# DeltaNet: the keys' sums of squares from their transposed copy; last FFN: 512 tokens in one PSUM bank

## The chip, the cores and the metric

The program runs on one core of one Trainium2 chip. The metric is device time in microseconds (us), the median of the runs shown. An execution taken by the hardware profiler gives the views quoted here: PE is TensorE (matmuls), PEld its weight loads, DVE is VectorE, ACT is ScalarE, POOL is GpSimd, SP is SyncE, which issues the DMAs. L12 is line 12 of the kernel before.

## The reference, cut to what matters

512 tokens of width 1024 pass through a first block of two layers (retention, sparse attention, gated MLP, each layer with a feed-forward network, FFN) and a second block of two layers. In the second block the first layer mixes with a gated DeltaNet over the 512 tokens and 256 context tokens, the second with differential attention; each is followed by an FFN. The context is dropped after the first of these layers, so the last FFN sees the 512 tokens alone. Two pieces matter here:

```
def _l2norm(x):
    return xf * lax.rsqrt(jnp.sum(jnp.square(xf), axis=-1, keepdims=True) + RMS_EPS)

# DeltaNet, per head of 128 channels, q, k, v after a 5-tap convolution and silu:
q = _l2norm(q) * (DN_DK ** -0.5);  k = _l2norm(k)

# FFN, hidden width 2816:
def _swiglu(h, w_gate, w_up, w_down):
    return (jax.nn.silu(h @ w_gate) * (h @ w_up)) @ w_down
```

## The kernel before, in words

All activations lie transposed, channels on the 128 partitions and tokens along the free axis. Every large product is made of three matmuls (`mm3`, L208 to L212): both operands are split into a high and a low fp32r part, and hi·hi, lo·hi and hi·lo are summed in PSUM. `gemm_b` (L243 to L255) loads and splits one unit of weights (`load_split`, L196 to L206: a DMA, a copy on ACT, a subtraction on DVE), takes one PSUM bank for each segment of tokens in `segs`, and runs over the segments and, inside, over the contraction in steps of 128. A segment of 256 tokens is a matmul of 256 columns, one of 512 tokens a matmul of 512.

**The last FFN** (`ffn2`, L1408 to L1463, called by `rest` with `halves`, two segments of 256 tokens). The 2816 hidden channels are 22 chunks of 128, in three groups of 8, 8 and 6. `gate_up` (L1415) makes one chunk: gate and up products, 8 contraction steps each, then tanh on ACT (L1429), two operations on DVE (L1430, L1431), the high part on ACT (L1432) and the low part on DVE (L1433), all once for each segment. `down` (L1435) makes one of the 8 output chunks from a group's hidden chunks and adds it into x (L1439). The first four chunks are made half by half, since each half's input comes out of a layer norm of its own, and the third group's `down` is made half by half, since the layer norm behind it wants each half complete. In between, chunks 4 to 21 and the `down` of groups 1 and 2 run over both halves in one call, as two segments. This phase has six PSUM banks for the products and two for statistics. In the built program's memory layout the FFN's input tiles (`ghhi`, `ghlo`) begin at multiples of 64 bytes, as do those of the first block's FFN (`fhhi`, `fhlo`) and all hidden tiles (`ahi`, `alo`, `bhi`, `blo`); the inputs of the second block's first FFN (`ahhi`, `ahlo`) begin 32 bytes past one.

**The DeltaNet's projection** (`project` in `dn`, L1020 to L1057), once for each of 8 heads and for k, q and v in this order: products, a copy to SBUF, a 5-tap convolution on DVE (L1036), silu by tanh on ACT (L1037, tile `cth`) and one operation on DVE (L1038), which leaves `kT`, `qT` or `vT`, channels by 768 tokens with 4 columns of padding. For q and k the squares are taken on ACT (L1042, tile `sq`, which shares the one buffer of `cth`), and for each of six token tiles a matmul against a column of ones sums them over the partitions into one PSUM bank (L1045, `pss`); DVE adds 1e-6 (L1047, `vvk`, `vvq`). For k and v six transposes on TensorE, three to a bank, and two copies, one on DVE and one on ACT (L442, L276, L274), make the token-major `ktok` and `vtok`. `pss` and the transposes share one PSUM bank (tag "t"). `blocks` (L1059) takes the reciprocal roots on POOL (`rk`, `rq`, L279) and builds the decay-weighted products, `invert` the triangular inverses, `scan` the recurrence. Two heads are projected ahead of the one that is scanned.

The order of instructions on each engine is set when the program is built, by the Tile framework's scheduler, from the order of the code, the waits and a priority that the weight loads and `invert` carry. Each engine then runs its list in order.

Of the kernel before, what the change touches and what calls it, by code (L numbers as in the profile page):

```python
# [14 lines left out]
F32 = mybir.dt.float32  # L15
F32R = mybir.dt.float32r
AF = mybir.ActivationFunctionType
OP = mybir.AluOpType
AX = mybir.AxisListType
# [3 lines left out]
P = 128  # L23
T = 512
# [163 lines left out]
class Kern:  # L188
# [723 lines left out]
    def dn(self, then):  # L912


        tc, nc, a = self.tc, self.nc, self.a
        nt, n, PAD = 6, NALL, 4
        both = ((0, NCTX, 1, a["ctxT"]), (NCTX, T, 0, self.xd[:]))
        W_ = n + PAD
        col0 = lambda t: t * P + (PAD if t >= 2 else 0)
        tsl = lambda t: slice(col0(t), col0(t) + P)  # L920
        segs = ((0, NCTX), (NCTX, T))
        with ExitStack() as pools:
# [17 lines left out]
            with tc.tile_pool(name="dg", bufs=1, reuse_waits="tile") as dg:  # L940
# [23 lines left out]
                y, e, z, z2, p, g = (dg.tile([P, nt, 16], F32, name=x) for x in ("y", "e", "z", "z2", "p", "g"))  # L964
# [19 lines left out]
                for t in range(nt):  # L984
                    for d in range(2):
                        nc.tensor.matmul(pc[:, (t * 2 + d) * 8:(t * 2 + d) * 8 + 8], tri[d], g[:, t, d * 8:d * 8 + 8],
                                         start=True, stop=True)
# [18 lines left out]
            dq = pools.enter_context(tc.tile_pool(name="dq", bufs=1, reuse_waits="tile"))  # L1006
            dr = pools.enter_context(tc.tile_pool(name="dr", bufs=1, reuse_waits="tile"))
# [12 lines left out]
            def project(hd):  # L1020

                hh = {}
                for nm in "kqv":
                    c = {"q": 0, "k": 8, "v": 16}[nm] + hd
                    pss_ = self.gemm_b(hk, KD, a["dn_in"][c], segs)
                    s = dq.tile([P, W_], F32, name=f"{nm}T", bufs=DNB[nm])
                    hh[nm + "T"] = s
                    th = dr.tile([P, W_], F32, name="cth", bufs=1)
                    cp = cps[flip[0] % 2]
                    flip[0] += 1  # L1030
                    for (s0, w), ps in zip(segs, pss_):
                        c0 = col0(s0 // P)
                        nc.scalar.activation(cp[:, c0 + 2:c0 + 2 + w], ps[:, :w], AF.Copy)
                    nc.scalar.activation(s, cp[:, 2:2 + W_], AF.Copy, scale=self.conv[:, c, 2:3])
                    for j in (0, 1, 3, 4):
                        nc.vector.scalar_tensor_tensor(s, cp[:, j:j + W_], self.conv[:, c, j:j + 1], s, op0=OP.mult, op1=OP.add)  # L1036
                    nc.scalar.activation(th, s, AF.Tanh, scale=0.5)  # L1037
                    nc.vector.scalar_tensor_tensor(s, th, 1.0, s, op0=OP.add, op1=OP.mult)  # L1038
                    if nm != "v":

                        sq = dr.tile([P, W_], F32, name="sq", tag="cth", bufs=1)
                        nc.scalar.activation(sq, s, AF.Square, scale=0.5)  # L1042
                        pq = self.ps("t", "pss")
                        for t in range(nt):
                            nc.tensor.matmul(pq[:, t:t + 1], sq[:, tsl(t)], self.ones[:, 0:1], start=True, stop=True)  # L1045
                        vv = dq.tile([P, nt], F32, name=f"vv{nm}", bufs=3)
                        nc.vector.tensor_scalar(vv, pq[:, :nt], 1e-6, None, op0=OP.add)  # L1047
                        hh["vv" + nm] = vv
                    if nm != "q":
                        tok = dq.tile([P, nt, P], F32, name=f"{nm}tok", bufs=DNB[nm + "tok"])  # L1050
                        hh[nm] = tok
                        for t0 in (0, 3):
                            pt = self.ps("t", "qkvt")
                            for t in range(3):
                                self.tpose(pt[:, t * P:(t + 1) * P], s[:, tsl(t0 + t)])
                            self.copy(tok[:, t0:t0 + 3].rearrange("p t c -> p (t c)"), pt[:, :3 * P])
                return hh  # L1057

            def blocks(hh, hd):  # L1059
# [211 lines left out]

            ah = DNB["ahead"]
            hs = {i: project(i) for i in range(ah)}
            w = blocks(hs[0], 0)
            invert(w)
            zs = {i: z_gate(i) for i in range(ZA)}
            for hd in range(8):
                w0 = w
                for step in ORD:
                    if step == "z" and hd < 8 - ZA:  # L1280
                        zs[hd + ZA] = z_gate(hd + ZA)
                    elif step == "s":
                        with (tc.high_priority() if HP & 2 else nullcontext()):
                            scan(hs[hd], hd, w0, zs.pop(hd))
                    elif step == "b" and hd < 7:
                        with (tc.high_priority() if HP & 4 else nullcontext()):
                            w = blocks(hs[hd + 1], hd + 1)
                    elif step == "i" and hd < 7:
                        with (tc.high_priority() if HP & 1 else nullcontext()):
                            invert(w)  # L1290
                    elif step == "p" and hd + ah < 8:
                        hs[hd + ah] = project(hd + ah)
# [115 lines left out]
    def ffn2(self, l, n, x, f, fp, norm):  # L1408

        nc, a = self.nc, self.a  # L1410
        streams, h = f["streams"], f["h"]
        hk = lambda k: (h[0][:, k], h[1][:, k])
        act = {}

        def gate_up(c, part, by_k=False):  # L1415
            segs = tuple(p[:2] for p in part)
            ws = a["f_gate"][l, c], a["f_up"][l, c]
            if by_k:
                pg, pu = self.gemm_k(hk, KD, ws, segs)
            else:  # L1420
                pg, pu = (self.gemm_b(hk, KD, w, segs) for w in ws)
            if c not in act:
                act[c] = [fp.tile([P, n], F32R, name=f"b{s}", tag=f"b{s}", bufs=10) for s in ("hi", "lo")]
            hi, lo = act[c]
            for (s0, w, _), g_, u_ in zip(part, pg, pu):
                s = slice(s0, s0 + w)
                th = fp.tile([P, 512], F32, name="bth", bufs=2)
                g = fp.tile([P, 512], F32, name="bg", bufs=2)
                nc.scalar.activation(th[:, :w], g_[:, :w], AF.Tanh, scale=0.5)  # L1429
                nc.vector.scalar_tensor_tensor(g[:, :w], th[:, :w], 1.0, g_[:, :w], op0=OP.add, op1=OP.mult)  # L1430
                nc.vector.scalar_tensor_tensor(g[:, :w], g[:, :w], 0.5, u_[:, :w], op0=OP.mult, op1=OP.mult)  # L1431
                nc.scalar.activation(hi[:, s], g[:, :w], AF.Copy)  # L1432
                nc.vector.tensor_tensor(lo[:, s], g[:, :w], hi[:, s], op=OP.subtract)  # L1433

        def down(gi, c0, cn, m, part):  # L1435
            ps = self.gemm_b(lambda k: act[c0 + k], cn, a[f"f_down{gi}"][l, m], tuple(p[:2] for p in part))
            for (s0, w, st), p in zip(part, ps):
                xs = x[:, m, s0:s0 + w]
                nc.vector.scalar_tensor_tensor(xs, p[:, :w], self.mod[:, l, st, 40 + m:41 + m], xs, op0=OP.mult, op1=OP.add)  # L1439
                yield xs  # L1440

        for gi, (c0, cn) in enumerate(GROUPS):
            if gi == 0:

                for p in streams:
                    for c in range(NLEAD):
                        gate_up(c, [p], c == 0)

                ag = f["ag"]
                for k in range(KD):  # L1450
                    nc.scalar.activation(x[:, k], x[:, k], AF.Identity, scale=ag[:, 0, k:k + 1], bias=ag[:, 1, k:k + 1])
            for c in range(max(c0, NLEAD), c0 + cn):
                gate_up(c, streams)
            if gi < 2:
                for m in range(KD):
                    for _ in down(gi, c0, cn, m, streams):
                        pass
            else:
                for i, p in enumerate(streams):
                    st = self.ln_begin(p[1], i)  # L1460
                    for m in range(KD):
                        for xs in down(gi, c0, cn, m, [p]):
                            self.ln_add(st, xs)  # L1463
                    norm(i, self.ln_end(st))
# [246 lines left out]
```

## Time and profile before

| what | us |
|---|---|
| median of 3 runs (lowest, highest) | 3587.92 (3581.33, 3589.96) |
| the profiled execution | 3586.47 |
| its span, from the first to the last instruction | 3584.7 |
| PE busy | 3429.6 |
| DVE busy | 2183.5 |
| ACT busy | 1450.8 |

The profiled execution lies 1.45 us under the median; 1.77 us of it lie outside the span. Matmuls are pipelined, so a matmul's own duration overlaps the next one's; the step from one matmul's start to the next is what it costs in a dense stream. "Granted clock" is the share of TensorE's full clock, 1.00 for 2.4 GHz and 0.50 for 1.2 GHz.

### The profile page before, as it was taken

How to read it: one execution, taken by the hardware profiler on the slowest of the kernel's cores; microseconds unless marked ns; L12 is line 12 of the kernel's file. 1: busy time of each engine (PE TensorE's matmuls, PEld its weight loads, DVE VectorE, ACT ScalarE, POOL GpSimd, SP SyncE). 2: the span in 40 equal slices, each digit the busy share in tenths (PEclk: the TensorE clock that was granted, in tenths of full speed). 3: DMA queues.
4: the chain of work that ended last, by engine and by line, in shares of the span. 5: the costliest groups of instructions: out<-in, count | busy, mean ns of one | idle time of the engine just before them, and what ended most of it. 6: DMA issues, size and time to landing. Idle time of an engine off the chain costs nothing.

```text
span 3584.7 us, 57586 instructions
## 1 busy us (share of the span) xinstructions
PE 3429.6 (96%) x23334; PEld 2890.0 (81%) x23334; DVE 2183.5 (61%) x4509; ACT 1450.8 (40%) x2736; POOL 119.2 (3%) x125
## 2 busy tenths in 40 slices
PE   8999999989999999999999899999998999989998
PEld 7677888876778888787888777888888877679998
DVE  4556995545569844586778676333247666674446
ACT  4442322335333222556666755112126444452224
POOL 1000000010000000000100000000000000000000
PEclk9998999999989999999999799999999999999999
DMA  5113563330125833211111232111123211133223
GB/s 194 50 52 102 188 222 123 113 96 34 57 101 200 268 113 121 92 54 34 54 47 33 65 104 100 65 65 60 65 81 112 74 42 46 58 124 107 95 94 108
DMA packets 119859, 341.60 MB, mean 95 GB/s; under 512 B 16865, under 2 KB 33521, under 8 KB 119080
## 3 DMA queue, kind: packets, MB, share of 16 engines
q1 hardware_dynamic: 119592, 337.92, 28.5%
q8 instruction: 183, 3.00, 0.3%
q14 instruction: 84, 0.69, 0.1%
HBM read 326.26 MB, written 14.75 MB: 95 GB/s over the span
## 4 chain that ended last, share of the span: by engine, by line
PE 79%; DVE 8%; ACT 5%; DMA 3%; issue 2%; POOL 2%; SPq 0%; POOLq 0%; DVEq 0%; ACTq 0%
PE gb L210 17%; PE gb L212 17%; PE gb L211 17%; DMA wada<-ada_w 2%; PE S L1562 2%; PE ga L210 2%; PE ga L212 2%; DVE wlo L205 2%; PE ga L211 2%; PE S L611 1%; PE da L212 1%; PE da L211 1%; PE da L210 1%; ACT whi L204 1%; PE po L637 1%
## 5 line engine op out<-in xcount | busy, mean ns | idle before, releaser
L204 ACT ACTIVATE whi<-wraw 128x1024 fp32r<-128x1024 f32 (+3 forms) x513 | 490.6, 957 | 1204.6 <-PE gb L211 881.0
L205 DVE TENSOR_TENSOR wlo<-wraw,whi 128x1024 fp32r<-128x1024 f32 (+3 forms) x513 | 561.6, 1096 | 388.7 <-ACT whi L204 384.3
L210 PE MATMUL gb<-fhhi,whi 128*128 128x512 f32 x704 | 275.8, 392 | 3.2 <-ACT fhhi L317 3.2
L212 PE MATMUL gb<-fhhi,wlo 128*128 128x512 f32 x704 | 275.8, 392 | 2.0 <-DVE wlo L205 1.8
L211 PE MATMUL gb<-fhlo,whi 128*128 128x512 f32 x704 | 275.5, 391 | 0.0
L210 PE MATMUL gb<-ahhi,whi 128*128 128x256 f32 (+1 forms) x672 | 226.8, 337 | 0.7 <-ACT whi L204 0.7
L211 PE MATMUL gb<-ahlo,whi 128*128 128x256 f32 (+1 forms) x672 | 226.5, 337 | 0.0
L212 PE MATMUL gb<-ahhi,wlo 128*128 128x256 f32 (+1 forms) x672 | 226.3, 337 | 0.0
L211 PE MATMUL gb<-blo,whi 128*128 128x256 f32 (+1 forms) x704 | 218.3, 310 | 0.0
L210 PE MATMUL gb<-bhi,whi 128*128 128x256 f32 (+1 forms) x704 | 218.2, 310 | 0.0
L212 PE MATMUL gb<-bhi,wlo 128*128 128x256 f32 (+1 forms) x704 | 218.2, 310 | 0.0
L893 DVE CUSTOM_DVE_ANT_0 ada_t<-wada,ada_s 128x1024 f32<-128x1024 f32 x160 | 195.2, 1220 | 19.7 <-DMA wada<-ada_w 18.2
L210 PE MATMUL gb<-dhhi,whi 128*128 128x256 f32 (+1 forms) x528 | 192.3, 369 | 7.6 <-ACT dhhi L909 7.4
L211 PE MATMUL gb<-dhlo,whi 128*128 128x256 f32 (+1 forms) x528 | 192.5, 365 | 0.3 <-DVE dhlo L910 0.3
L212 PE MATMUL gb<-dhhi,wlo 128*128 128x256 f32 (+1 forms) x528 | 192.2, 365 | 0.0
L210 PE MATMUL gb<-ghhi,whi 128*128 128x256 f32 x672 | 188.4, 280 | 2.6 <-ACT whi L204 2.6
L211 PE MATMUL gb<-ghlo,whi 128*128 128x256 f32 x672 | 187.7, 279 | 0.0
L212 PE MATMUL gb<-ghhi,wlo 128*128 128x256 f32 x672 | 187.6, 280 | 0.0
L210 PE MATMUL ga<-whi,hhi 128*128 128x384 f32 (+2 forms) x448 | 164.6, 367 | 14.3 <-ACT hhi L317 10.7
L211 PE MATMUL ga<-wlo,hhi 128*128 128x384 f32 (+2 forms) x448 | 163.8, 366 | 3.3 <-DVE wlo L205 3.3
L212 PE MATMUL ga<-whi,hlo 128*128 128x384 f32 (+2 forms) x448 | 163.8, 366 | 0.0
L210 PEld LDWEIGHTS gb<-fhhi,whi 128*128 128x128 f32 x704 | 133.2, 189 | 31.4 <-ACT fhhi L317 4.0
(510 smaller groups left out, 8501.0 us busy)
## 6 DMA issues: line engine op xcount, KB each, us to landing
wada<-ada_w SPq DMA_DIRECT2D x96, 512.0 KB, 4.3
wraw<-f_gate SPq DMA_DIRECT2D x52, 512.0 KB, 3.2
wraw<-f_up SPq DMA_DIRECT2D x52, 512.0 KB, 3.3
wraw<-w_gate SPq DMA_DIRECT2D x44, 512.0 KB, 4.0
wraw<-w_up SPq DMA_DIRECT2D x44, 512.0 KB, 3.7
wraw<-da_in SPq DMA_DIRECT2D x40, 512.0 KB, 3.2
wraw<-w_down SPq DMA_DIRECT2D x32, 512.0 KB, 3.3
wraw<-dn_in SPq DMA_DIRECT2D x32, 512.0 KB, 3.4
```

The lines of the kernel that those rows point to most:

```text
L204: nc.scalar.activation(hi[:, :n], raw[:, :n], AF.Copy)
L205: nc.vector.tensor_tensor(lo[:, :n], raw[:, :n], hi[:, :n], op=OP.subtract)
L210: nc.tensor.matmul(out, l[0], r[0], start=start, stop=False)
L211: nc.tensor.matmul(out, l[0], r[1], start=False, stop=False)
L212: nc.tensor.matmul(out, l[1], r[0], start=False, stop=stop)
L611: nc.tensor.matmul(ps[:, :n], qT[s, p, t * P:(t + 1) * P], kT[s, b, :n], start=True, stop=True)
L637: nc.tensor.matmul(po[64 * g:64 * g + 64, j * P:], vt[:, j, b * P + 64 * g:b * P + 64 * g + 64], pts[g][:, :n], start=b == 0 and j == 0, s ...
L893: nc.vector.tensor_tensor_reduce(th, w, s[:, st], 0.5, 0.0, op0=OP.mult, op1=OP.add, accum_out=self.mod[:, l, st, f:f + 1])
L1562: nc.tensor.matmul(ps[:, k0:k0 + kn], qT[s, i, t * P:(t + 1) * P], kx, start=True, stop=True)
```

## The change

In the last FFN, where the two halves belong to one stream and together fit 512 columns, chunks 4 to 21 and the `down` of groups 1 and 2 take one segment of 512 tokens in place of two of 256. In the DeltaNet the keys' squares are taken from `ktok`, on ACT as before, and summed on DVE by one reduction along the free axis; the queries keep the matmuls against ones. The tile `sq` of the keys is written after the copies of `ktok`, and still in the buffer of `cth`.

```
-                    if nm != "v":
+                    if nm == "q":
                         sq = dr.tile([P, W_], F32, name="sq", tag="cth", bufs=1)
                         nc.scalar.activation(sq, s, AF.Square, scale=0.5)
-                        pq = self.ps("t", "pss")
+                        ss = self.ps("t", "pss")
                         for t in range(nt):
-                            nc.tensor.matmul(pq[:, t:t + 1], sq[:, tsl(t)], self.ones[:, 0:1], start=True, stop=True)
-                        vv = dq.tile([P, nt], F32, name=f"vv{nm}", bufs=3)
-                        nc.vector.tensor_scalar(vv, pq[:, :nt], 1e-6, None, op0=OP.add)
-                        hh["vv" + nm] = vv
-                    if nm != "q":
+                            nc.tensor.matmul(ss[:, t:t + 1], sq[:, tsl(t)], self.ones[:, 0:1], start=True, stop=True)
+                    else:
                         tok = dq.tile([P, nt, P], F32, name=f"{nm}tok", bufs=DNB[nm + "tok"])
...
+                    if nm == "k":
+                        ss = dr.tile([P, nt], F32, name="ssk", bufs=2)
+                        sq = dr.tile([P, W_], F32, name="sq", tag="cth", bufs=1)[:, :n]
+                        nc.scalar.activation(sq, tok[:].rearrange("p t c -> p (t c)"), AF.Square, scale=0.5)
+                        nc.vector.tensor_reduce(ss, sq.rearrange("p (t c) -> p t c", c=P), axis=AX.X, op=OP.add)
+                    if nm != "v":
+                        vv = dq.tile([P, nt], F32, name=f"vv{nm}", bufs=3)
+                        nc.vector.tensor_scalar(vv, ss[:, :nt], 1e-6, None, op0=OP.add)
+                        hh["vv" + nm] = vv
...
+        whole = streams
+        if len({p[2] for p in streams}) == 1 and n <= T:
+            whole = ((streams[0][0], n, streams[0][2]),)
...
             for c in range(max(c0, NLEAD), c0 + cn):
-                gate_up(c, streams)
+                gate_up(c, whole)
             if gi < 2:
                 for m in range(KD):
-                    for _ in down(gi, c0, cn, m, streams):
+                    for _ in down(gi, c0, cn, m, whole):
                         pass
```

The built order shows where the instructions went. On ACT, in the projection of the first head, before (`cth` is the tanh, `sq` the square, `cp` a copy of products):

```order
L1037 ACTIVATE cth<-kT 128x772
L1033 ACTIVATE cp_11332<-gb_11777 128x256
L1033 ACTIVATE cp_11332<-gb_11778 128x512
L1034 ACTIVATE vT<-cp_11332,c_dn_conv 128x772
L1042 ACTIVATE sq<-kT 128x772
L1033 ACTIVATE cp_11333<-gb_11855 128x256
L1037 ACTIVATE cth<-qT 128x772
L274 ACTIVATE ktok<-qkvt 128x384
L1042 ACTIVATE sq<-qT 128x772
```

and now:

```order
L1037 ACTIVATE cth<-kT 128x772
L1033 ACTIVATE cp_11332<-gb_11772 128x256
L1033 ACTIVATE cp_11332<-gb_11773 128x512
L1034 ACTIVATE vT<-cp_11332,c_dn_conv 128x772
L1033 ACTIVATE cp_11333<-gb_11850 128x256
L274 ACTIVATE ktok<-qkvt 128x384
L1058 ACTIVATE sq<-ktok 128x768
L1037 ACTIVATE cth<-qT 128x772
L204 ACTIVATE whi<-wraw 128x1024
L1033 ACTIVATE cp_11333<-gb_11851 128x512
L1042 ACTIVATE sq<-qT 128x772
```

The keys' square moved behind the copy of `ktok`, and the queries' tanh, which needs the same buffer, behind both. On DVE, at the same place, now (before, no reduction stood here, and `vvk` was read out of the bank `pss`):

```order
L1038 SCALAR_TENSOR_TENSOR kT<-cth,kT 128x772
L1036 SCALAR_TENSOR_TENSOR qT<-cp_11333,c_dn_conv,qT 128x772
L276 COPY ktok<-qkvt 128x384
L1036 SCALAR_TENSOR_TENSOR vT<-cp_11332,c_dn_conv,vT 128x772
L1101 SCALAR_TENSOR_TENSOR gam<-grow,Gc,c_minmask 128x128
L1036 SCALAR_TENSOR_TENSOR vT<-cp_11332,c_dn_conv,vT 128x772
L1059 TENSOR_REDUCE ssk<-sq 128x6
L1036 SCALAR_TENSOR_TENSOR vT<-cp_11332,c_dn_conv,vT 128x772
L1062 TENSOR_SCALAR vvk<-ssk 128x6
L1038 SCALAR_TENSOR_TENSOR qT<-cth,qT 128x772
```

The reduction and `vvk` stand ahead of the queries' silu. On ACT, at the last chunk of the last FFN, before:

```order
L1429 ACTIVATE bth<-gb_32576 128x256
L204 ACTIVATE whi<-wraw 128x768
L1429 ACTIVATE bth<-gb_32577 128x256
L1432 ACTIVATE bhi<-bg 128x256
L204 ACTIVATE whi<-wraw 128x768
L1432 ACTIVATE bhi<-bg 128x256
```

and now:

```order
L204 ACTIVATE whi<-wraw 128x768
L1436 ACTIVATE bth<-gb_31151 128x512
L204 ACTIVATE whi<-wraw 128x768
L1439 ACTIVATE bhi<-bg 128x512
L204 ACTIVATE whi<-wraw 128x768
```

One tanh and one high part of 512 columns stand in the place of two of 256 each.

## Rows read from the trace of the kernel before

**Rows 1.** Page, parts 1 and 4: busy time, and the chain's shares by engine.
```profile
PE 3429.6 (96%) x23334; PEld 2890.0 (81%) x23334; DVE 2183.5 (61%) x4509; ACT 1450.8 (40%) x2736; POOL 119.2 (3%) x125
...
PE 79%; DVE 8%; ACT 5%; DMA 3%; issue 2%; POOL 2%; SPq 0%; POOLq 0%; DVEq 0%; ACTq 0%
```
**Rows 2.** Sums by stretch, last FFN: stretch, length, busy by engine (count), granted clock, DMA.
```profile
core 0: us, PE busy (x) PEld busy (x) DVE busy (x) ACT busy (x) POOL busy (x), PEclk, DMA share, GB/s
...
3300.00:3340.00 40.00, 40.00 (x338) 40.00 (x337) 15.62 (x23) 8.83 (x12) 0.00 (x0) 1.00 0.27 93
```
**Rows 3.** Timeline of PE, last FFN, gate and up: start, duration; first and 87th.
```profile
3339.82 0.28 PE L211 MATMUL gb<-ghlo,whi 128*128 128x256 f32 x1
...
3349.95 0.28 PE L210 MATMUL gb<-ghhi,whi 128*128 128x256 f32 x1
```
**Rows 4.** Timeline of PE, last FFN, down: first and 79th matmul of a dense stretch.
```profile
3299.53 0.28 PE L212 MATMUL gb<-bhi,wlo 128*128 128x256 f32 x1
...
3308.89 0.28 PE L212 MATMUL gb<-bhi,wlo 128*128 128x256 f32 x1
```
**Rows 5.** Timeline of PE, first block's FFN, 512 columns: first and 19th matmul.
```profile
499.75 0.39 PE L210 MATMUL gb<-fhhi,whi 128*128 128x512 f32 x1
...
503.83 0.39 PE L210 MATMUL gb<-fhhi,whi 128*128 128x512 f32 x1
```
**Rows 6.** Timeline of PE, second block's first FFN: 18 of 256, then 24 of 512.
```profile
2364.48 0.28 PE L210 MATMUL gb<-ahhi,whi 128*128 128x256 f32 x1
...
2366.46 0.28 PE L212 MATMUL gb<-ahhi,wlo 128*128 128x256 f32 x1
2366.58 0.40 PE L210 MATMUL gb<-ahhi,whi 128*128 128x512 f32 x1
...
2371.95 0.39 PE L212 MATMUL gb<-ahhi,wlo 128*128 128x512 f32 x1
```
**Rows 7.** Groups by form: busy, mean ns | idle before, releaser; first block's hidden tiles, 512 columns.
```profile
L211 PEld LDWEIGHTS gb<-alo,whi 128*128 128x128 f32 x352 | 66.1, 188 | 14.8 <-DVE alo L823 1.3
```
**Rows 8.** Sums by stretch, DeltaNet, columns as in rows 2: start, eight heads, end.
```profile
1490.00:1573.00 83.00, 80.49 (x748) 70.00 (x747) 72.23 (x174) 43.55 (x63) 7.67 (x6) 0.96 0.22 65
1573.00:2010.00 437.00, 406.74 (x5194) 352.14 (x5192) 330.59 (x926) 291.69 (x635) 37.74 (x45) 0.95 0.13 40
2010.00:2095.00 85.00, 74.19 (x822) 62.30 (x822) 52.36 (x146) 51.55 (x141) 3.07 (x3) 0.81 0.26 82
```
**Rows 9.** Chain that ended last, 1490 to 2095: shares by line; then one piece.
```profile
by line: PE gb L210 9.6%; PE gb L211 9.5%; PE gb L212 9.3%; issue 4.2%; ACT Nd L1126 4.1%; PE p L1241 4.1%; PE pss L1045 3.6%; PE p L1246 3.6%; PE p L1228 3.5%; ACT DU L1170 3.5%; PE p L1226 2.8%; ACT DT L1170 2.8%; PE p L1230 2.3%; PE py L
...
1740.26 1.24 PE pss L1045 x12
```
**Rows 10.** The tile `sq`, 1490 to 2095: ns min/median/max; then who waited for it.
```profile
L1042 ACT ACTIVATE sq<-kT x8: 832/840/874, 1493.2 to 1954.6; 128x772 f32<-128x772 f32 x8
...
  ACT cth L1037: 4.8, 3
```
**Rows 11.** Reductions of DVE by line: ns min/median/max, first and last start, forms.
```profile
L666 DVE TENSOR_REDUCE ss<-sq x16: 414/481/552, 231.2 to 1028.9; 128x4 f32<-128x256 f32 x8, 128x6 f32<-128x384 f32 x8
...
L1564 DVE TENSOR_REDUCE mx<-S x64: 943/956/959, 2826.0 to 3119.6; 128x1 f32<-128x768 f32 x64
```
**Rows 12.** Timeline of ACT, first and third head's projection: start, duration, [idle before].
```profile
1496.44 0.85 ACT L1037 ACTIVATE cth<-qT 128x772 f32<-128x772 f32 x1 [2.09 <-PE pss L1045]
1499.01 0.49 ACT L274 ACTIVATE ktok<-qkvt 128x384 f32<-128x384 f32 x1 [1.73 <-PE qkvt L442]
...
1585.98 0.85 ACT L1037 ACTIVATE cth<-qT 128x772 f32<-128x772 f32 x1 [2.35 <-PE pss L1045]
...
1592.46 0.49 ACT L274 ACTIVATE ktok<-qkvt 128x384 f32<-128x384 f32 x1
```
**Rows 13.** The same, last head.
```profile
1962.08 0.49 ACT L274 ACTIVATE ktok<-qkvt 128x384 f32<-128x384 f32 x1 [1.10 <-PE qkvt L442]
...
1979.11 0.85 ACT L1037 ACTIVATE cth<-qT 128x772 f32<-128x772 f32 x1
```

## The prediction

> **What bounds the kernel now.** Start with the page: TensorE is busy 96% of the span and takes 79% of the chain that ended last, against 61% and 8% for DVE [rows 1]. Such a share is an average, so each stage that the change touches is read by itself.
>
> In the last FFN the sums by stretch show TensorE busy in every microsecond, at a granted clock of 1.00 (2.4 GHz), with DVE at 15.6 and ACT at 8.8 us of 40 and the DMAs at 0.27 [rows 2]. Nothing there waits for anything but TensorE, so the stage costs its number of matmuls times the step from one start to the next. That step is read from the timeline, by first row, last row and count. Gate and up at 256 columns: 3349.95 - 3339.82 = 10.13 us over 86 steps, 117.8 ns [rows 3]. Down at 256 columns: 9.36 us over 78 steps, 120.0 ns [rows 4]. At 512 columns the first block's FFN takes 4.08 us over 18 steps, 226.7 ns [rows 5]. A matmul of double width therefore costs less than two.
>
> The DeltaNet is another kind of stage. TensorE is busy 80.5, 406.7 and 74.2 us of its three stretches, 561 of 605 in all, DVE 455 [rows 8]. TensorE leads, but small products wait there for ACT and DVE and back. The chain through it names the summing matmuls L1045 with 3.6% of 605 us, 21.8 us, in pieces of twelve records of about 1.24 us [rows 9].
>
> **The FFN, part by part.** Merged are chunks 4 to 21 in gate and up: 18 x 2 products x 8 steps x 3 matmuls = 864 pairs. Each pair of 2 x 117.8 = 235.6 ns becomes one of 226.7: 8.9 ns, together 7.7 us. In the down products it is 8 output chunks x 16 hidden chunks x 3 = 384 pairs: 240.0 - 226.7 = 13.3 ns, together 5.1 us. Sum: 12.8 us, all of it on the path.
>
> The step at 512 columns is the open price. The second block's first FFN runs its 256 columns at 1.98 us over 17 steps, 116.5 ns, and its 512 columns at 5.37 us over 23, 233.5 ns, twice as much [rows 6]. At that price gate and up would gain 235.6 - 233.5 = 2.1 ns a pair, 1.8 us, and the FFN 1.8 + 5.1 = 6.9; with the down products at 233.5 too (6.5 ns a pair, 2.5 us) it would be 4.3. I take 226.7: the products on tiles that begin at multiples of 64 bytes show that step, and the tiles of the last FFN do, while the inputs that show 233.5 begin 32 bytes past one. The lower end is kept for the range.
>
> Evictions halve in number and double in width. DVE and ACT lose a little and are hidden by their idle time [rows 2]. Weight loads and DMAs keep their number. One place loses cover: behind chunk 21 the first `down` by halves needs that chunk's high part after 15 matmuls of 120 ns, 1.8 us, and now a chain of 512 columns leads to it. In the first block, where all this runs at 512 columns, weight loads waited 1.3 us for low parts in the whole kernel [rows 7], and the built order puts four matmuls of the next output chunk ahead. I put down 0.3 us, between 0 and 1.6.
>
> **The DeltaNet, part by part.** Removed are 8 groups of six sums, 8 x 1.24 = 9.9 us of TensorE [rows 9], and a use of the bank they share with the transposes. The square stays on ACT (0.84 us, now 768 in place of 772 columns [rows 10]). Added are 8 reductions on DVE of 768 to 6. No such shape is in the trace; 768 to 1 takes 0.956 us, and 384 to 6 took 0.552 [rows 11], so 0.95 us each, 7.6 us on DVE. The small `vvk` stays.
>
> Added too is a wait. The queries' tanh needs the buffer that the keys' square occupies, so it now comes behind the transposes, both copies, the square and the reduction, where it had come behind six sums. That earlier wait cost ACT 4.8 us in all [rows 10], 2.09 and 2.35 of it in the first and third head [rows 12]. In the last head the second copy starts at 1962.08 and the tanh only at 1979.11 [rows 13]: the new chain of 0.5 + 0.84 + 0.95 fits, as it does in five heads of eight. In the first head the tanh would move from 1496.44 to about 1501.3, in the third from 1585.98 to about 1594.7 [rows 12]. Queued behind it on ACT are copies of products and the recurrence's small copies; the built order has already moved it behind some of these. The queries' products are needed a head later, and TensorE has other projections to run.
>
> What this is worth is bounded by 9.9 us at the top (all of it on the path) and by a loss of 7.6 us (the DVE work all on the path, the TensorE work all filled by waits). TensorE is the busier engine, so I take half of the upper end, 5.0 us gained.
>
> **The sum:** 3586.5 (the profiled execution, 1.45 us under the median) - 12.8 + 0.3 - 5.0 = 3569.0 us, 17.5 less. The stages lie apart, so the parts add.
>
> The Trainium skill, "VectorE: DVE Perf Modes", section "Rules for kernel authors", calls tensor_reduce on a hot path the slowest DVE operation and advises to restructure; this change moves towards it. By that rule the move is a loss; the first rival below is its price here.
>
> **Rivals.** *VectorE takes back what TensorE gives.* For it: DVE is busy 72 of 83 us in the first stretch [rows 8], where the first head's inverse waits for its results. Against: over the eight heads it has 106 us of 437 free. Then the DeltaNet ends between 0 and 4 us later and the kernel at 3574 to 3578.
>
> *The width saves little.* If gate and up follow rows 6, the FFN gives 6.9 us, and with half of the DeltaNet's gain the kernel ends near 3575; with the down products following too, near 3577.5. The Trainium skill, "TensorE: Matmul & The Clock Gate", section "Back-to-back issue gap", gives N/2.4 + 2.5 ns for the step, so 2.6 ns a pair and an estimate of 3.2 us for the FFN. By that the kernel would end near 3579, by an estimate; rows 3 and 4 against rows 5 show 8.9 and 13.3 ns a pair.
>
> *The built order turns out worse.* Most instructions of the DeltaNet moved a place or two. If it gives back 5 to 15 us, the end is 3579 to 3589.
>
> *Slower: the single buffer holds the heads up.* If in each head the queries' tanh waits in ACT's queue for the reduction, and the recurrence's copies behind it wait too, TensorE idles, and its clock can fall as it does at the end of this stage (0.81, [rows 8]). The price is the first head's lateness in rows 12, 4.9 us, in each of eight heads: 40 us, less 9.9 and 12.5, 17 us slower, about 3604. It decides from (10.8 + 12.5 + 9.9) / 8 = 4.2 us a head. Against it: five heads have room as in rows 13.
>
> That the change doesn't do what it says is excluded by the built order: the wide forms and the reductions stand there.
>
> **Chances.** A change of 0.3%, 10.8 us, is about what can be told from none; faster therefore means under 3577.2. The sum as it stands: 0.57. VectorE's rival: 0.17, of which 0.13 faster. Little from the width: 0.06, of which 0.04 faster. A worse order: 0.13, all within 0.3%. The slow rival: 0.04. More than half from the DeltaNet, below 3564: 0.03. That gives faster 0.77, same 0.19, slower 0.04. The range runs from 3561, where the DeltaNet gives its whole 9.9 and a little on the wait removed from ACT, to 3580, where it gives back some 6; about 0.12 lie above and 0.05 below.
>
> **What would show it.** In the profile after: gate and up on `ghhi` with 512 columns at steps near 227 ns, the stretch from chunk 4 to the third group's down shorter by 12 to 13 us with TensorE still busy throughout; 96 records of L1045 where 192 were; 8 reductions near 0.95 us; the DeltaNet's stretch some 5 us shorter. Steps near 234 prove the first term wrong. A DeltaNet stretch that is no shorter, with DVE or ACT as releaser of TensorE more often than now, proves the second wrong; a longer one with the tanh L1037 waiting for DVE is the slow rival.

## The result, and the profile after

The changed kernel takes 3563.36 us (median of 4 runs, 3560.42 to 3570.49), the kernel before, timed beside it, 3585.90 (3581.33 to 3589.96): a ratio of 0.994, 95% interval 0.9921 to 0.996. It is faster by about 0.6%. The forecast was 3569.0 with 3561 to 3580 as its range. The profiled execution of the changed kernel took 3570.49, against 3586.47 before: 16.0 us less where the sum had 17.5. By the medians it is 22.5 us: the profiled execution is the slowest of the changed kernel's four, the one before lies near its median.

The page, parts 1 and 4, answers to [rows 1]. TensorE lost 24 us of busy time and 1344 matmul records (864 + 384 merged, 96 records of the sums gone, twelve for each group of six), and DVE moved up in the chain.

```profile
PE 3405.6 (95%) x21990; PEld 2819.5 (79%) x21990; DVE 2178.1 (61%) x4447; ACT 1443.6 (40%) x2700; POOL 120.9 (3%) x125
...
PE 74%; DVE 11%; ACT 5%; DMA 4%; issue 3%; POOL 2%; SPq 0%; POOLq 0%; DVEq 0%; ACTq 0%
```

To see where the time went, both traces are cut at marks that both have: the first tanh of kT (1490.75 us before, 1490.78 after), the first matmul on the second block's FFN input `ahhi`, and in the last FFN the first wide matmul and the third group's `down`. The sums by stretch of the kernel before, from the tanh of the first kT to the second block's FFN (columns as in [rows 2]):

```profile
1490.75:2146.60 655.85, 610.34 (x7017) 525.45 (x7017) 498.28 (x1355) 414.00 (x898) 49.55 (x55) 0.93 0.18 56
```

And after: the same stretch, 40 us inside the last FFN, and from the first wide matmul there to the third group's `down`:

```profile
1490.78:2139.53 648.75, 597.36 (x6922) 513.94 (x6920) 504.40 (x1363) 413.51 (x898) 51.91 (x55) 0.93 0.18 56
...
3280.00:3320.00 40.00, 40.00 (x178) 33.06 (x177) 14.89 (x15) 7.43 (x7) 0.00 (x0) 1.00 0.29 92
...
3229.26:3514.20 284.94, 284.94 (x1250) 234.33 (x1249) 108.92 (x122) 72.92 (x89) 0.00 (x0) 1.00 0.31 96
```

The first row is what answers to [rows 8]: the DeltaNet's stretch is 7.1 us shorter, with 13 us less of TensorE and 6 us more of DVE. The second answers to [rows 2]: still busy throughout at a granted clock of 1.00, with 178 matmuls where 338 were. From the first matmul on `ghhi` to the third group's `down` the last FFN takes 344.2 us (3169.99 to 3514.20) where it took 354.6 (3175.39 to 3529.95), 10.4 less. Between the two stretches 1.7 us came back: in the mixer pass ahead of the last FFN the granted clock was 0.50 from 3162 to 3166 us, where it had been 1.00 throughout before. So 7.1 + 10.4 - 1.7 = 15.8 of the 16.0.

The timeline of PE after, gate and up (first and 52nd of a dense stretch), which answers to [rows 3]:

```profile
3344.95 0.39 PE L210 MATMUL gb<-ghhi,whi 128*128 128x512 f32 x1
...
3356.63 0.39 PE L210 MATMUL gb<-ghhi,whi 128*128 128x512 f32 x1
```

That is 11.68 us over 51 steps, 229.0 ns, neither the 226.7 of [rows 5] nor the 233.5 of [rows 6]. The `down` products of group 1, 192 matmuls from 3273.22 to the next gate at 3316.78, take 43.56 us, 226.9 ns each.

The new reduction, by its tile, and then ACT at the first, third and last head, which answers to [rows 12, 13]:

```profile
L1059 DVE TENSOR_REDUCE ssk<-sq x8: 932/950/955, 1497.0 to 1960.8; 128x6 f32<-128x768 f32 x8
...
  ACT cth L1037: 1.0, 1
```
```profile
1497.94 0.85 ACT L1037 ACTIVATE cth<-qT 128x772 f32<-128x772 f32 x1 [1.02 <-DVE ssk L1059]
...
1594.89 0.84 ACT L1037 ACTIVATE cth<-qT 128x772 f32<-128x772 f32 x1
...
1964.20 0.85 ACT L1037 ACTIVATE cth<-qT 128x772 f32<-128x772 f32 x1 [1.57 <-DVE qT L1036]
```

The reduction takes 0.95 us, as put down, and ACT waited for it once, 1.0 us in all. The queries' tanh of the third head stands at 1594.89, where 1594.7 was expected, that of the first at 1497.94, where the prediction had 1501.3. In the last head it even came 15 us earlier than before (1979.11 in [rows 13]). L1045 has 96 records, and 7 pieces in the chain through this stretch where 17 were before.

### The profile page after: what moved, and what is told of

It is laid out like the page before. It is cut to its first block, busy times and chain, and to the rows that moved or that the text cites. A ratio compares the mean times of both kernels' runs of the same rounds, so it can differ in the third digit from the quotient of the medians.

```text
span 3568.7 us, 54752 instructions
## 1 busy us (share of the span) xinstructions
PE 3405.6 (95%) x21990; PEld 2819.5 (79%) x21990; DVE 2178.1 (61%) x4447; ACT 1443.6 (40%) x2700; POOL 120.9 (3%) x125
## 4 chain that ended last, share of the span: by engine, by line
PE 74%; DVE 11%; ACT 5%; DMA 4%; issue 3%; POOL 2%; SPq 0%; POOLq 0%; DVEq 0%; ACTq 0%
PE gb L210 16%; PE gb L212 16%; PE gb L211 16%; DMA wada<-ada_w 3%; DVE wlo L205 2%; PE S L1573 2%; DVE ada_t L893 2%; PE ga L212 2%; PE ga L210 2%; PE ga L211 2%; PE da L212 1%; PE da L211 1%; PE da L210 1%; PE S L611 1%; ACT whi L204 1%
## 5 line engine op out<-in xcount | busy, mean ns | idle before, releaser
L210 PE MATMUL gb<-ahhi,whi 128*128 128x256 f32 (+1 forms) x672 | 226.7, 337 | 0.7 <-ACT whi L204 0.7
L893 DVE CUSTOM_DVE_ANT_0 ada_t<-wada,ada_s 128x1024 f32<-128x1024 f32 x160 | 195.4, 1221 | 23.3 <-DMA wada<-ada_w 21.8
L211 PE MATMUL gb<-blo,whi 128*128 128x512 f32 (+1 forms) x576 | 195.8, 340 | 0.0
L212 PE MATMUL gb<-bhi,wlo 128*128 128x512 f32 (+1 forms) x576 | 195.6, 340 | 0.0
L210 PE MATMUL gb<-bhi,whi 128*128 128x512 f32 (+1 forms) x576 | 195.4, 340 | 0.0
L212 PEld LDWEIGHTS gb<-fhhi,wlo 128*128 128x128 f32 x704 | 133.0, 189 | 34.7 <-DVE wlo L205 7.2
L211 PEld LDWEIGHTS gb<-fhlo,whi 128*128 128x128 f32 x704 | 133.1, 189 | 27.7
L210 PE MATMUL da<-whi,ahhi 128*128 128x256 f32 x512 | 149.0, 291 | 0.0
```

The lines of the kernel that those rows point to most:

```text
L210: nc.tensor.matmul(out, l[0], r[0], start=start, stop=False)
L211: nc.tensor.matmul(out, l[0], r[1], start=False, stop=False)
L212: nc.tensor.matmul(out, l[1], r[0], start=False, stop=stop)
L893: nc.vector.tensor_tensor_reduce(th, w, s[:, st], 0.5, 0.0, op0=OP.mult, op1=OP.add, accum_out=self.mod[:, l, st, f:f + 1])
```

## The experiments

Each is timed in five rounds beside the kernel before. "Stretch" is the DeltaNet's, as cut above. The five built kernels that keep the changed DeltaNet (after, e2, e3, e4, and e8, which only moves its input tile) run its operations on ACT and DVE in one and the same order, by their traces, and give the spread between executions: 648.8, 646.4, 646.1, 641.7 and 646.0 us, mean 645.8. In them TensorE is busy for 591.4 to 601.7 us, 597.8 in the mean, and idle for 44.6 to 51.4, 48.0 in the mean. With the old DeltaNet (before, e1) the stretch is 655.9 and 655.0, mean 655.4. The change is worth 9.6 us there. Single executions of the same work differ by up to 7.1 us, so a smaller difference between two of them says nothing by itself.

**e1, the last FFN alone.** The kernel before, with

```
+        whole = streams
+        if len({p[2] for p in streams}) == 1 and n <= T:
+            whole = ((streams[0][0], n, streams[0][2]),)
...
-                gate_up(c, streams)
+                gate_up(c, whole)
...
-                    for _ in down(gi, c0, cn, m, streams):
+                    for _ in down(gi, c0, cn, m, whole):
```

> The kernel before with the wide segment in the last FFN alone; the DeltaNet is as before. Mark the last FFN by the first matmul on ghhi and the first matmul of the third group's down: 354.6 us before, 344.2 after the whole change. If the FFN's part is all width (gate and up 864 pairs at 228.9 in place of 235.6 ns, 5.8 us; down 384 pairs at 226.9 in place of 240.0, 5.0 us; a stall of 0.4 back), the stretch is again 344.2 and the time falls by 10.4 us, a ratio of 0.997. Rival: the two parts of the change touch (the order that the whole change built is better also here); then the stretch is longer than 346 or the time falls by less than 8 us. The DeltaNet, from the first tanh of kT to the first matmul on the second block's FFN input (655.9 us before), should stay within 1 us of that.

Ratio 0.9971 (0.9959 to 0.9983), the 10.4 us expected of 3586. The last FFN's stretch is 343.2 us, its wide part 284.90 (284.94 after), the DeltaNet 655.0.

**e2, the DeltaNet alone.** The changed kernel with `streams` put back for `whole` in those two calls.

> The kernel before with the keys' sums from ktok alone; the last FFN runs halves. The DeltaNet from the first tanh of kT to the first matmul on the second block's FFN input took 655.9 us before and 648.8 after the whole change. If that gain belongs to the moved sums, this kernel shows 648.8 +- 1 and a time 7.1 us shorter, a ratio of 0.998; with the FFN's 10.4 that makes 17.5 of the 22.5 us between the medians. Rival: part of the gain is chance of one execution; then the stretch lies nearer to 655.9 and the time falls by less than 4 us.

Ratio 0.9977 (0.9963 to 0.9990), 8.2 us. The stretch is 646.4, where 648.8 give or take 1 was expected, and the last FFN's is 355.0. The parts add: 10.4 + 8.2 = 18.6 us, inside the interval of the whole change (14 to 28 us).

**e3 and e4, the input tiles moved by 32 and by 64 bytes.** Ahead of `ghhi` and `ghlo`, in e3 (16 columns in e4):

```
+                pad = fp.tile([P, 8], F32, name="ghpad")
+                nc.vector.memset(pad, 0.0)
```

> The changed kernel with a pad of 32 bytes ahead of ghhi and ghlo, so that both begin 32 bytes past a multiple of 64, as ahhi and ahlo do. Place theory (the step of a wide matmul hangs on where its moving tile lies): gate and up rise from 228.9 to about 233.5 ns a pair, the stretch from the first wide matmul on ghhi to the third group's down from 284.9 to 288.9 us, and the whole is 4.0 us slower than the changed kernel, less whatever the narrow matmuls of the first four chunks gain (117.8 to 116.5 ns, 0.5 us). Rival (the step hangs on what runs beside the matmuls, evictions and transfers, or on the stage): 228.9 and 284.9 stay.

> The changed kernel with a pad of 64 bytes ahead of ghhi and ghlo: they now begin 64 bytes past a multiple of 128, as fhhi, bhi and blo do, where they had begun at one. If the place of the moving tile by 128 bytes is what separates 228.9 ns (ghhi, ghlo) from 227.0 (fhhi, bhi), gate and up come to 227.0 a pair, the stretch from the first wide matmul to the third group's down to 283.3 us, 1.6 less than the changed kernel, and narrow matmuls of the first four chunks from 117.8 to about 120 ns. Rival (stage, not place): 228.9 and 284.9 stay.

PE's timeline, gate and up, first and 52nd of a dense stretch, of e3:

```profile
3329.78 0.39 PE L211 MATMUL gb<-ghlo,whi 128*128 128x512 f32 x1
...
3341.68 0.39 PE L211 MATMUL gb<-ghlo,whi 128*128 128x512 f32 x1
```

and of e4:

```profile
3309.81 0.39 PE L212 MATMUL gb<-ghhi,wlo 128*128 128x512 f32 x1
...
3321.66 0.40 PE L212 MATMUL gb<-ghhi,wlo 128*128 128x512 f32 x1
```

e3: 11.90 us over 51 steps, 233.3 ns, as the place theory has it. Its wide stretch came to 291.2 us, more than the 288.9 expected, because the pad also moved `bhi` and `blo`, which stand behind it: their 192 matmuls took 44.80 us, 233.3 ns in place of 226.9. 864 x 4.4 and 384 x 6.4 ns make the 6.3 us. So in this stage the place of the moving tile decides. The narrow matmuls of the first four chunks, which were to fall to 116.5 ns, did not: their median step is 119. e4 missed: 11.85 us over 51, 232.4 ns, where 227.0 was expected; the `down` products on `bhi` and `blo` rose to 228.9 (43.95 us over 192), and the stretch to 288.7. The offset within 128 bytes is not the rule. Both kernels stay faster than the kernel before, at 0.9965 (0.9948 to 0.9982) and 0.9959 (0.9940 to 0.9978).

**e8, all moving tiles of the second block at the offset that was fast.** Pads in four places; for the last FFN:

```
+                nc.gpsimd.memset(fp.tile([P, 48], F32, name="gpad"), 0.0)
+                gh = [fp.tile([P, KD, T], F32R, name=f"gh{s}") for s in ("hi", "lo")]
+                nc.gpsimd.memset(fp.tile([P, 80], F32, name="bpad"), 0.0)
```

> The changed kernel with pads that put every moving tile of the second block (dhhi, ahhi, ghhi, bhi, the mixers' mhi and their low parts) 64 bytes past a multiple of 512, where fhhi, ahi and bhi lie that show 227 ns at 512 columns. Place theory, refined (the two shifts gave, by the offset in 256 bytes: 64: 227; 128: 228.9; 192: 232.4; 96 and 160: 233.4): ahhi at 512 columns falls from 233.5 to 227 (1056 pairs, 6.9 us) and rises at 256 from 117 to 119 or 120 (1056 pairs, 2 to 3 us back), so the stretch of the second block's first FFN (582.3 us) loses 4 to 5; ghhi falls from 228.9 to 227.0 (1.6 us, first wide matmul to third down 283.3); dhhi at 512 columns falls by up to 7 ns, 792 pairs, at most 5 us of the DeltaNet. Some 6 to 10 us less in all than the changed kernel. Rival (the offset only shifts cost between forms, or the tiles' distance from something else sets it): no stage shorter by over 2 us.

The timeline of PE in e8, first and 52nd matmul of gate and up of the last FFN:

```profile
3329.65 0.39 PE L211 MATMUL gb<-ghlo,whi 128*128 128x512 f32 x1
...
3341.21 0.39 PE L211 MATMUL gb<-ghlo,whi 128*128 128x512 f32 x1
```

and its sums by stretch, the second block's first FFN and the last FFN's wide part:

```profile
2133.15:2711.90 578.75, 567.56 (x3249) 498.30 (x3248) 249.00 (x385) 165.06 (x246) 2.71 (x3) 0.99 0.25 76
3215.84:3498.75 282.91, 282.91 (x1251) 234.24 (x1250) 108.85 (x122) 72.91 (x89) 0.00 (x0) 1.00 0.31 97
```

11.56 us over 51 steps is 226.7 ns, the value of [rows 5], now for the last FFN too. Its wide part is 2.0 us shorter, the first FFN 3.1 (581.8 after): its matmuls of 512 fell to 228.0 ns in the mean (all steps under 330 ns) and those of 256 rose from 118.8 to 121.4. The DeltaNet missed: its 646.0 shows no gain, and the median step on `dhhi` at 512 columns only went from 235 to 233 ns. Ratio 0.9915 (0.9893 to 0.9937), median 3553.1: the fastest version of this study, though its interval still meets that of the changed kernel (0.9921 to 0.996); 5.1 us are shown by the stretches.

**e5, e6 and e7: the DeltaNet's sums, ordered anew.** e5 takes the keys' squares from `kT` again and sums them by matmuls, but behind the transposes; e6 adds a second reduction; e7, shown here, leaves the keys' sums out and takes a constant for the norm:

```
-                        ss = dr.tile([P, nt], F32, name="ssk", bufs=2)
...
+                        ss = self.ones
...
-                        nc.vector.tensor_scalar(vv, ss[:, :nt], 1e-6, None, op0=OP.add)
+                        nc.vector.tensor_scalar(vv, ss[:, :nt], 1e6 if nm == "k" else 1.0, 1e-6, op0=OP.mult, op1=OP.add)
```

> The changed kernel, but the keys' squares come from kT again and are summed by matmuls against ones into the bank pss; only their place is new, behind the transposes and copies of ktok. The DeltaNet's stretch was 655.9 and 655.0 us in the two executions with the sums ahead of the transposes, and 641.7 to 648.8 (mean 645.7) in four executions with the change: some 9.7 us. Theory 1 (the sums' own 8 x 1.24 = 9.9 us of TensorE lay on the path): the sums are back, so the stretch is again about 655. Theory 2 (what cost was that the keys' transposes stood behind the sums and the addition that empties their bank, so ktok came late): the stretch stays near 646.

> The changed kernel with the keys' reduction done twice over, the second over the first's result: 8 x 0.95 = 7.6 us more on VectorE and as much later on the queries' tanh, nothing on TensorE. If VectorE's work is hidden, as the measured gain of some 9.7 us in place of my 5.0 suggests, the DeltaNet's stretch stays between 641 and 650 us. Rival (VectorE pays for it one for one): 645.7 + 7.6 = 653.

> The changed kernel without the keys' squares and sums: a constant stands in their place, so ACT's 8 squares (0.84 us), VectorE's 8 reductions (0.95 us) and the waits on the buffer they shared are gone. This is the floor for every way of making these sums. If nothing of the new work lies on the path, the DeltaNet's stretch stays at 641 to 650 us; if the single buffer or VectorE still holds the heads up, it falls to 640 or below, up to 8 x (0.84 + 0.95) = 14.3 us under 645.7.

| kernel | ratio (interval) | stretch, us | granted clock in it |
|---|---|---|---|
| e5 | 1.0009 (0.9994 to 1.0025) | 668.4 | 0.91 |
| e6 | 1.0025 (1.0008 to 1.0042) | 675.1 | 0.90 |
| e7 | 0.9973 (0.9955 to 0.9990) | 659.2 | 0.91 |

The sums by stretch, of e5, e6 and e7:

```profile
1486.13:2154.57 668.44, 623.73 (x7017) 534.73 (x7017) 499.42 (x1355) 412.29 (x898) 51.00 (x55) 0.91 0.19 54
...
1490.55:2165.61 675.06, 615.89 (x6921) 529.21 (x6921) 510.43 (x1369) 411.73 (x895) 50.84 (x55) 0.90 0.18 54
...
1489.56:2148.73 659.17, 607.46 (x6904) 521.21 (x6905) 495.52 (x1343) 407.00 (x889) 46.10 (x53) 0.91 0.19 55
```

None fits any theory as it was put. The kernel with no key sums at all is 13 us slower in this stretch than the one with them, and 7.6 us more on DVE cost 29. Length less TensorE's busy time is its idle time: 44.7, 59.2 and 51.7 us. Only e6 waits clearly longer than the five executions above; e7 lost 10 us, and e5 all of its loss, to a TensorE that was busy longer. What all three have in common is that the scheduler, given other durations and waits, ordered the DeltaNet's instructions anew on every engine. What was tested was the order as much as the work, so the next four hold the order fixed.

**e9 to e12: the same order.** The order of every engine in one built kernel is written down, and given to the scheduler of another as an edge from each instruction to the next:

```
+        for a, b in zip(seq, seq[1:]):
...
+            tc.add_manual_dep(b, a.name, mybir.DependencyInfo(mybir.DependencyClass.NoSync, mybir.DependencyReason.DATA), reason="order")
```

e9, e10 and e11 have the changed kernel's order, e12 that of e6, in the whole program. e9 cuts the square and the reduction from 768 columns to 12 and takes a constant for the norm, so it leaves the keys' sums out:

```
-nc.scalar.activation(sq, tok[:].rearrange("p t c -> p (t c)"), AF.Square, scale=0.5)
-nc.vector.tensor_reduce(ss, sq.rearrange("p (t c) -> p t c", c=P), axis=AX.X, op=OP.add)
+nc.scalar.activation(sq[:, :2 * nt], tok[:, 0, :2 * nt], AF.Square, scale=0.5)
+nc.vector.tensor_reduce(ss, sq[:, :2 * nt].rearrange("p (t c) -> p t c", c=2), axis=AX.X, op=OP.add)
```

e10 halves the squares and reads each of them twice:

```
+nc.vector.tensor_reduce(ss, sq.rearrange("p (t c) -> p t c", c=P).unsqueeze(2).to_broadcast([P, nt, 2, P]), axis=AX.XY, op=OP.add)
```

e11 puts six matmuls a head back ahead of the keys' transposes, on `kT` itself, in a bank of the same tag; nothing reads them, and they alone stand outside the held order (`EXTRA`):

```
+                            more = self.ps("t", "pss")
+                            for t in range(nt):
+                                EXTRA.append(nc.tensor.matmul(more[:, t:t + 1], s[:, tsl(t)], self.ones[:, 0:1], start=True, stop=True).ins.name)
```

and e12 changes no instruction, only the order.

> The changed kernel's built order, held instruction by instruction on every engine, with the keys' sums taken out of the work: the square takes 12 columns in place of 768 and the reduction 12 in place of 768, a constant stands in for the norm. About 8 x (0.65 + 0.8) us less on ACT and VectorE, the same waits, nothing else. Work theory: what the DeltaNet's stretch gains or loses is the work that is moved; then it falls under the five executions of the changed kernel's order (641.7 to 648.8 us, mean 645.8), by up to 11 us. Order theory (the built order decides; the kernel without key sums took 659.2 us because the scheduler ordered everything anew): it stays at 641 to 649, and well under 659.

> The changed kernel's built order, held, with the keys' reduction of double length in one instruction (each square read twice, halved ahead): 8 x about 0.9 us more on VectorE and nothing else. The kernel with a second reduction, ordered anew, took 675.1 us. Order theory: 645.8 plus at most 7.2 us, likeliest 646 to 650. Work theory (VectorE's extra work costs several times its length): 660 or more.

> The changed kernel's built order, held, with six matmuls of kT against ones per head back on TensorE ahead of the keys' transposes, in a bank of the same tag, 8 x 1.24 = 9.9 us; nobody reads them. This prices the removed sums by themselves. If they lie on the path: 645.8 + 9.9 = 655.7, as long as the kernel before (655.0, 655.9), and the DeltaNet's gain is the removed TensorE work. If they are hidden by waits: 642 to 649, and the gain is the order's. Half, as I took it: 651.

> The changed kernel's own work, every instruction of it, held in the order that the scheduler built for the kernel with the second reduction (675.1 us), less that second reduction. Order theory: most of the 29 us stay, the stretch is 665 or more, and the kernel is slower than before at 1.000 to 1.003. Work theory: without the second reductions it is back at 642 to 650.

The DeltaNet's stretch in the sums by stretch, of e9:

```profile
1491.78:2139.18 647.40, 598.79 (x6922) 514.91 (x6921) 498.74 (x1363) 408.40 (x898) 51.73 (x55) 0.93 0.19 56
```

of e10:

```profile
1493.82:2144.53 650.71, 601.53 (x6921) 517.23 (x6921) 510.20 (x1363) 413.95 (x898) 51.93 (x55) 0.93 0.18 56
```

of e11:

```profile
1488.61:2149.47 660.86, 612.98 (x7018) 528.72 (x7017) 504.87 (x1363) 413.96 (x898) 51.93 (x55) 0.93 0.18 55
```

and of e12:

```profile
1490.36:2158.55 668.19, 608.12 (x6922) 521.78 (x6922) 504.16 (x1361) 411.28 (x895) 50.85 (x55) 0.92 0.18 54
```

One of e11's eight groups, with the matmuls before and behind it:

```profile
1668.68 0.28 PE L212 MATMUL gb<-dhhi,wlo 128*128 128x256 f32 x1
1668.80 1.41 PE L1050 MATMUL pss<-ones,kT 128*128 128x1 f32 x12
1670.27 0.55 PE L442 MATMUL qkvt<-c_ident,kT 128*128 128x128 f32 x3
```

Compare DVE's busy time and the length, each with the changed kernel's 504.4 and 645.8. e9 has 6 us less on DVE and 5 less on ACT, and is as long: 647.4, ratio 0.9942 (0.9924 to 0.9960). e10 has 6 more on DVE (its reduction takes 1.75 us) and ratio 0.9940 (0.9921 to 0.9960), that of the changed kernel; its 650.7 leaves room for at most part of those 6 us. VectorE's reduction is hidden, or nearly. (The unaltered work in its own order, held, was not run; that e9 and e10 have the changed kernel's ratio shows that the edges cost little.) e11 has the 96 matmul records back: 15 us longer than the mean, and ratio 0.9977 (0.9962 to 0.9991), with a median 10 to 13 us above those of e9 and e10. Its TensorE is idle for 47.9 us, as long as in the five executions, and busy for 613.0, 15 us longer: the sums filled no wait. Nor did they wait for their bank: TensorE goes into them from the matmul before without a pause. By the rows above a group takes 1.47 us up to the next matmul; seven take 1.33 to 1.47 and one, at a granted clock of 0.50, 2.78, together 12.9 us. So the sums lie wholly on the path, and cost somewhat more than the 9.9 us put down. e12 does the changed kernel's own work in 668.2 us, ratio 1.0025 (1.0010 to 1.0040): another order costs 22 us here, and turns the change into a loss. Its median lies some 30 us above those of e9 and e10, because that order also costs 9 to 10 us between this stretch and the last FFN (1037.9 us, against 1029.1 and 1028.3 in e9 and e10).

Of the 22 us, 12 are TensorE's idle time (60.1 us against 48.0 in the mean), and 10 its busy time (608.1 against 597.8) for the same matmuls at a granted clock of 0.92. Where it waits shows in this stretch of e12:

```profile
PE py L1182 <- ACT DT L1177: 11.6, 12, 3.2
...
PE p L1248 <- DVE zT L1017: 5.7, 1, 5.7
```

and of the changed kernel:

```profile
PE py L1182 <- ACT DT L1177: 4.6, 9, 1.0
```

The columns are us in all, times, longest. In e12 the inverse's products wait 7 us longer for ACT, and once 5.7 us for `zT`, whose gate shares the buffer `cth`; in the changed kernel that wait is not among the eleven largest.

## Why the prediction was right, and where its steps were not

The direction, the range and the two places where the time comes from were right. Two terms were off, in opposite directions: the FFN gave about 2 us less than put down, the DeltaNet 4.6 more. That the sum came as near as it did is in part luck.

*The FFN, -12.8 + 0.3.* Measured -10.4, up to the third group's `down`. The mechanism holds: the stage is bound by TensorE throughout [rows 2], and the wide step is less than two narrow ones. The down products were right: 226.9 ns where 226.7 was put down, 384 x 13.1 ns = 5.0 us. The term that was mis-sized is gate and up: 228.9 ns in the mean over the 864, so 6.7 ns a pair and 5.8 us, not 8.9 and 7.7. The reason given for 226.7, that tiles at multiples of 64 bytes show it, is right in kind (e3, e8) and wrong as a rule: `ghhi` begins at a multiple of 64 in the changed kernel and in e4, and shows 228.9 and 232.4. The stall behind chunk 21 comes after this stretch: four steps of 190 to 225 ns among the first 39 of the third `down`, where steps of 120 stood, 0.36 us where 0.3 was put down.

*The DeltaNet, -5.0.* Measured -9.6 (means of the executions named above). The step that failed is "I take half of the upper end", taken because TensorE is only the busier of two engines there. With the order held, the work of VectorE is free between nothing and double (e9, e10), and the matmuls cost all of their 9.9 us and more, with no wait that they fill (e11). The chain of waits had said so: L1045 held 21.8 us of it [rows 9] for 16 groups, 10.9 for the keys' eight. That was quoted and then halved. The case called "more than half from the DeltaNet, below 3564", with a chance of 0.03, is where the median came to lie.

*The rivals.* "VectorE takes back what TensorE gives" is out by e10: the rule of the Trainium skill, "VectorE: DVE Perf Modes", section "Rules for kernel authors", against tensor_reduce on a hot path did not bite, because the 0.95 us were not on the path. "The width saves little" was partly right, for gate and up. The Trainium skill, "TensorE: Matmul & The Clock Gate", section "Back-to-back issue gap", gives N/2.4 + 2.5 ns for an isolated matmul and says itself that a stream of weight loads and matmuls is spaced otherwise; the prediction took the formula for such a stream, and 2.6 ns a pair should have been 2.5. These streams show 6.7 and 13.1 ns saved, and a step that moves by 6.6 ns with the place of the operand. "Slower: the single buffer" did not come: ACT waited 1.0 us for the reduction, and e9, which shortens the chain behind that buffer by 1.4 us a head, is no faster. A buffer of its own was not tried.

*The built order* was the rival to fear. It was given 5 to 15 us; e12 shows 22 in the DeltaNet, enough for a result above the kernel before. At equal work on TensorE the changed kernel's order is no better than the old one's: e11 takes 660.9 us, the kernel before 655.4 (one execution against two; by the runs, e11's 8.2 us gained against the 10.4 of its FFN, it is some 2 us worse). What the change gained is the work it took off TensorE, and the order did not take that back; no row of a trace prices an order, so this had to be run.

Left open: why e5, e6 and e7 ran at a granted clock of 0.90 or 0.91 over the stretch where the others show 0.92 to 0.95. In e6 longer waits may be the cause of the lower clock, or in part its result; e5 has no more idle time on TensorE (44.7 us) than the kernel before (45.5), so there longer waits do not explain it. Only e6's order was run with other work. How much of e11's 15 us beyond the 12.9 is the clock, and how much the spread of single executions, is open too.

## What to carry to other kernels

In a stage with small products, a stretch of TensorE on the chain can be worth its whole length, as it was here, and work moved to an engine that is busy 78% of the time can still be free: price each by the chain and by where it waits, not by splitting the difference of busy shares. Where a scheduler orders the program, an experiment that changes work changes the order too, and that can be worth more than the work; hold the order, then change one thing. Before a wide matmul is priced from another stage, compare where the moving tiles begin.

## What the runs showed that was not expected

- The step of a matmul hangs on where its moving tile begins. At 512 columns, by the offset of the tile in 256 bytes: 226.7 to 227 ns at 64 (`fhhi`, `bhi`, and in e8 `ghhi` and `ahhi`), 228.9 at 128 (`ghhi`; `bhi` in e4), 232.4 at 192 (`ghhi` in e4), 233.3 to 233.5 at 96 and 160 (`ahhi`; `bhi` and `ghhi` in e3). At 256 columns the ranking turns round: 120 at 64, 118 at 128, 117 at 96; at 160 and 192 (`ghhi` in e3 and e4) only the narrow matmuls of the first four chunks ran, with medians of 119 and 120. Of the rest only 224 stands in a kernel (`dhhi`), and why it is so stays open; in the DeltaNet, where `dhhi` stood at 64 in e8, the median step at 512 columns stayed at 233, so something else seems to count there.
- Five executions of the same DeltaNet took between 641.7 and 648.8 us, and the shortest is the one with the highest granted clock over the stretch (e4, 0.95 against 0.93).
- A reduction to 6 columns takes 0.158 us for 12 elements, 0.950 for 768 and 1.746 for 1536.
